# Decay logits of a gated linear attention: one float32r product on stacked high and low parts in place of a float32 product

## The chip, the core and the metric

The kernel runs on 1 core of one Trainium2 chip. The metric is the device time of one execution in microseconds (us), as the median of repeated runs; lower is better. The profile is one further execution, recorded by the hardware profiler. Its engines are PE (the matrix engine; PEld is its weight load), DVE (vector), ACT (scalar), POOL (GpSimd) and SP, which here only issues DMAs.

## The reference, cut to what matters

Two decoder layers work on 1024 tokens of width 1024. Each layer projects its normalised input to three groups of heads (windowed attention, retention, gated linear attention), gates their outputs, and projects back. The change touches only the decay of the gated linear attention: 16 low-rank channels `ga` of every token are multiplied by a 16 x 128 matrix, a bias is added, and the log-sigmoid of that is the log of the decay.

```
def hybrid_layer(x, c_act, positions, ...):
    h = rms_norm(x, pre_gain) * (1.0 + scale) + shift
    (aq, ak, av, ag, rq, rk, rv, rg, gq, gk, gv, gg, ga) = split(h @ w_in)
    ...
    gate_logits = ga @ gla_gate_w + gla_gate_b            # (1024, 16) @ (16, 128)
    log_a = log_sigmoid(gate_logits) / 16
    g = gated_linear_attention(gq, gk, gv, log_a)
    ...
    return x + gate * rms_norm(y, post_gain)
```

## The kernel before, in words

Tokens stand in 8 tiles of 128 (t = 0 to 7). A large product in float32 accuracy is made of three float32r products: both operands are split into a high part (rounded to float32r) and a low part (the rest), and high x high, low x high and high x low are added up in PSUM (`accum`, PASSES). Such matmuls all go through `mult` (L165); transposes go through `transp` (L180).

A layer begins with the gate stage. For each tile, `pre` (L651 to L708) squares the input on ACT, takes the power -1/2 on POOL (`rstd_of`, L634 on DVE and L635 on POOL), scales on DVE (L666), transposes on PE, and splits. Then `do_gates` projects the tile to the gate `gg` together with the 16 channels (272 columns) and to the gate `rg` (256 columns). In layer 0 this goes two tiles at a time, in layer 1 six and then two.

For each `gg` tile a job `gla_logits` (L990) copies the 16 channels from PSUM on ACT (L992), waits a planned time (`gz1`), transposes them on PE to 16 rows, and copies these to `gaT`, a tile of 32 rows x 512 tokens that POOL had set to ones (L781), so that row 16 is a row of ones for the bias. After four tiles a job `gla_log` (L1005) multiplies `gaT` by the weights `gwt` (16 rows of weights, a bias row, zeros): one float32 product of 32 rows x 128 columns with 512 moving columns, twice a layer, four times in all. ACT and DVE make the log-sigmoid of it (L1011 to L1016), and `gla_decays` (L1028) the decays.

`gwt` is a constant, set up before layer 0: DVE clears it (L805) and four DMAs on SP bring weights and bias of both layers (L807, L808).

What sets the order of the work: PE runs in the order in which the program issues its instructions. The small products are jobs (generators) that are resumed inside the long projections, after every 7th matmul (`pump`, CHUNK), when a planned clock `clk` has reached their time. `mult` adds a planned cost to this clock: for 512 columns 0.853 for float32 and 0.213 for float32r. So the planned cost of a product shifts what is issued behind it. The other engines' order is set by a list scheduler of the language. PSUM has three banks for projections (`mm`) and five for the rest (`aux`); SBUF tiles come from pools (`t1`: 8 buffers, `st` for weights on their way in: 5).

Other lines in the prediction: L533, L151 and L149 split loaded weights (low part on DVE or POOL, high part on DVE, high part on ACT); L364 adds up the modulation of the layer on DVE from loaded `w_mod` rows; L986 finishes SiLU of a gate on DVE and so frees the bank; L817 to L822 are the rotation of the retention's q and k on DVE.

Of the kernel before, what the change touches and what calls it, by code (L numbers as in the profile page):

```python
# [10 lines left out]
F32 = mybir.dt.float32  # L11
F32R = mybir.dt.float32r
I32 = mybir.dt.int32
AF = mybir.ActivationFunctionType
ALU = mybir.AluOpType
AX = mybir.AxisListType

P = 128
# [3 lines left out]
NT = S // P  # L22
# [71 lines left out]
def trunk(ctx: ExitStack, tc: tile.TileContext, ins, cst, out):  # L94
    nc = tc.nc
    V, A, G, T = nc.vector, nc.scalar, nc.gpsimd, nc.tensor
    x_in, c_in, pos_in, w_mod, b_mod, pre_g, post_g, w_in, sinks, gw_in, gb_in, gn_in, w_out, w_ga, w_last = [
        ins[n] for n in _INS
    ]

    cp = ctx.enter_context(tc.tile_pool(name="const", bufs=1))
    bp = ctx.enter_context(tc.tile_pool(name="big", bufs=1))
    gp = ctx.enter_context(tc.tile_pool(name="work", bufs=2))
# [5 lines left out]
    def nm(s):  # L109
        uid[0] += 1  # L110
        return f"{s}_{uid[0]}"
# [4 lines left out]
    def t1(dt=F32):  # L116
        return gp.tile([P, 256], dt, tag="t1", name=nm("t1"), bufs=B1)
# [4 lines left out]
    def small(w, dt=F32):  # L122
        return gp.tile([P, w], dt, tag="sm", name=nm("sm"), bufs=BS)
# [4 lines left out]
    def aux(dt=F32):  # L128
        return ps.tile([P, 512], dt, tag="aux", name=nm("aux"), bufs=8 - MMB)

    def f(ap):
        return ap.bitcast(F32)
# [20 lines left out]
    def dma(k, dst, src):  # L153
        {"S": nc.sync, "A": A, "P": G}[EN[k]].dma_start(dst, src)  # L154
# [24 lines left out]
    def transp(dst, src, idn):  # L179
        T.transpose(dst, src, idn)  # L180
        clk[0] += 0.056 if src.dtype == F32R else 0.109

    def lat(key, l):

        return L[key + "@1"] if l and key + "@1" in L else L[key]
# [4 lines left out]
    def flag(name, lat=0.0):  # L190
        flags[name] = clk[0] + lat
# [41 lines left out]
    def cload(name, dt=F32, eng=nc.sync):  # L233
        a = cst[name]
        t = cp.tile(list(a.shape), dt, name="c_" + name)
        eng.dma_start(t, a)
        return t
# [3 lines left out]
    ident = cload("ident", eng=A)  # L241
# [535 lines left out]
    gat = []  # L777

    def new_ga():
        gat.append(gp.tile([P, NT * P], F32, tag="kT1", name=nm("gaT"), bufs=1)[0:32, 0:512])  # L780
        G.memset(gat[-1], 1.0)  # L781
    stR = cp.tile([P, 2, P], F32, name="stR")
    stG = cp.tile([P, 4, 64], F32, name="stG")
    stC = cp.tile([P, 64], F32, name="stC")
# [16 lines left out]
    for l in range(DEPTH):  # L801
        V.tensor_copy(sink8[:, l].rearrange("p (m r) -> p m r", r=2),
                      sinkn[:, 8 * l:8 * l + 8].rearrange("p (r m) -> p m r", r=2))
    gwt = cp.tile([32, 2, P], F32, name="gwt")
    V.memset(gwt, 0.0)  # L805
    for l in range(DEPTH):
        nc.sync.dma_start(gwt[0:16, l, :], gw_in[l])  # L807
        nc.sync.dma_start(gwt[16:17, l, :], gb_in[l:l + 1, :])  # L808
    def rotary(dst, src, nh, t, kind):

        s4 = src.rearrange("p (h c k) -> p h c k", h=nh, c=2)
        sn = sincos[:, t, 0, kind * 32:kind * 32 + 32]
        cs = sincos[:, t, 1, kind * 32:kind * 32 + 32]
        b = gp.tile([P, 256], F32, tag="tr", name=nm("tr"), bufs=1)
        b4 = b[:, 0:nh * 64].rearrange("p (h c k) -> p h c k", h=nh, c=2)
        d4 = dst.rearrange("p (h c k) -> p h c k", h=nh, c=2)
        V.tensor_tensor(d4, s4, cs.unsqueeze(1).unsqueeze(1).to_broadcast((P, nh, 2, 32)), ALU.mult)  # L817
        snb = sn.unsqueeze(1).to_broadcast((P, nh, 32))
        V.tensor_tensor(b4[:, :, 0, :], s4[:, :, 1, :], snb, ALU.mult)
        V.tensor_tensor(b4[:, :, 1, :], s4[:, :, 0, :], snb, ALU.mult)  # L820
        V.tensor_tensor(d4[:, :, 0, :], d4[:, :, 0, :], b4[:, :, 0, :], ALU.subtract)
        V.tensor_tensor(d4[:, :, 1, :], d4[:, :, 1, :], b4[:, :, 1, :], ALU.add)  # L822
# [158 lines left out]
    def silu2(pg):  # L981

        th = t1()
        A.activation(th, pg, AF.Tanh, scale=0.5)
        sg = t1()
        V.scalar_tensor_tensor(sg, th, 1.0, pg, ALU.add, ALU.mult)  # L986
        return sg


    def gla_logits(l, t, pg, pa):  # L990
        ga = small(16)
        A.activation(ga, pa, AF.Copy)  # L992
        dma("ssg", sgS[t], silu2(pg))
        yield lat("gz1", l)
        if t >= 4:
            yield (0.0, ("z", l, 0))
        pt = aux()
        transp(pt[0:16, 0:P], ga, ident)
        A.activation(gat[l][0:16, (t % 4) * P:(t % 4 + 1) * P], pt[0:16, 0:P], AF.Copy)
        flag(("ga", l, t), lat("gz2", l))  # L1000

    las = {}
# [454 lines left out]
    def layer(l):  # L1457
        if l == 0:
            job(table_job())
        new_ga()  # L1460
        def do_gates(name, p):
            w = used(l, name)
            for t in (2 * p, 2 * p + 1):
                pg = mm()
                if name == "gg":
                    project(pg[:, 0:272], l, t, w, 272)
                    job(gla_logits(l, t, pg[:, 0:256], pg[:, 256:272]))
                else:
                    project(pg[:, 0:256], l, t, w)
                    dma("ssr", srS[t], silu2(pg[:, 0:256]))  # L1470
                pump()
            if p == NP_ - 1:
                load(l, "rk" if name == "gg" else "rv")
            if name == "gg" and p % 2:
                job(gla_log(l, p // 2))
# [237 lines left out]
```

## Time and profile before

| | |
|---|---|
| median of 3 runs | 1000.36 us (999.89 to 1002.28) |
| profiled execution, its own time | 1005.29 us |
| its span, first to last instruction | 1003.6 us |
| granted PE clock, mean | 0.989 |
| PE busy | 972.6 us (97%) |
| DVE, ACT, POOL busy | 683.7, 409.0, 234.7 us |
| DMA moved | 148.73 MB, mean 148 GB/s |

A line of a group reads: source line, engine, operation, tile written <- tiles read, shape, count | busy time in us, mean ns of one | idle time of the engine before them and what ended it. For PE the shape begins with the stationary operand, rows*columns. A line of a timeline reads: start, length in us, engine, line, operation, count, and in brackets the idle time before it.

### The profile page before, as it was taken

How to read it: one execution, taken by the hardware profiler on the slowest of the kernel's cores; microseconds unless marked ns; L12 is line 12 of the kernel's file. 1: busy time of each engine (PE TensorE's matmuls, PEld its weight loads, DVE VectorE, ACT ScalarE, POOL GpSimd, SP SyncE). 2: the span in 40 equal slices, each digit the busy share in tenths (PEclk: the TensorE clock that was granted, in tenths of full speed). 3: DMA queues.
4: the chain of work that ended last, by engine and by line, in shares of the span. 5: the costliest groups of instructions: out<-in, count | busy, mean ns of one | idle time of the engine just before them, and what ended most of it. 6: DMA issues, size and time to landing. Idle time of an engine off the chain costs nothing.

```text
span 1003.6 us, 19610 instructions
## 1 busy us (share of the span) xinstructions
PE 972.6 (97%) x7137; PEld 827.5 (82%) x7137; DVE 683.7 (68%) x1680; ACT 409.0 (41%) x1152; POOL 234.7 (23%) x275
## 2 busy tenths in 40 slices
PE   5899999999999999999999999999999999999896
PEld 1599999888998777778889999998999777777675
DVE  3788857678666778654677385775766577566786
ACT  2486312233332656632555332133333267563231
POOL 2310001223320234420122010122332034444000
PEclk8899999999999999999999999999999999999998
DMA  8842513623235355597555241352222435477883
GB/s 306 297 145 79 166 43 102 189 78 121 65 94 172 90 156 168 167 283 234 178 171 166 82 139 32 117 171 68 64 82 88 122 91 153 129 227 237 252 272 132
DMA packets 112172, 148.73 MB, mean 148 GB/s; under 512 B 11998, under 2 KB 63688, under 8 KB 112076
## 3 DMA queue, kind: packets, MB, share of 16 engines
q1 hardware_dynamic: 106380, 137.92, 44.2%
q10 hardware_dynamic: 5696, 9.56, 2.6%
q8 instruction: 56, 0.92, 0.4%
q14 instruction: 40, 0.33, 0.1%
HBM read 109.17 MB, written 36.18 MB: 145 GB/s over the span
## 4 chain that ended last, share of the span: by engine, by line
PE 80%; DMA 8%; DVE 7%; issue 2%; POOL 1%; ACT 1%; SPq 1%; ACTq 0%; POOLq 0%; DVEq 0%
PE mm L165 62%; PE aux L165 14%; PE aux L180 5%; DMA st<-in_w_in_dram 2%; DMA st<-in_w_last_dram 1%; POOL sm L635 1%; DMA xk<-in_x_dram 1%; DMA a<-mixS 1%; DMA t<-aoS 1%; DMA t<-mixF 1%; DVE arena L533 1%; DVE t L328 0%; SPq L154 0%; DMA t<-in_x_dram 0%; DMA t<-xs 0%
## 5 line engine op out<-in xcount | busy, mean ns | idle before, releaser
L165 PE MATMUL mm<-arena 128*128 128x256 f32 (+2 forms) x1824 | 300.0, 318 | 1.8 <-ACT arena L704 1.8
L165 PE MATMUL mm<-arena,arena 128*128 128x256 f32 (+2 forms) x1824 | 299.0, 317 | 0.0
L165 PEld LDWEIGHTS mm<-arena 128*128 128x128 f32 x1824 | 255.3, 191 | 26.6 <-issue 4.1
L165 PEld LDWEIGHTS mm<-arena,arena 128*128 128x128 f32 x1824 | 252.9, 188 | 25.2 <-issue 4.4
L635 POOL TENSOR_TENSOR sm<-sm,mhalf 128x1 f32<-128x1 f32 (+1 forms) x64 | 55.8, 871 | 347.0 <-DVE sm L634 328.4
L165 PE MATMUL mm<-arena,mx 128*128 128x512 f32 (+1 forms) x564 | 132.6, 392 | 3.7 <-ACT kept L1332 3.7
L165 PEld LDWEIGHTS mm<-arena,mx 128*128 128x128 f32 x564 | 103.0, 190 | 28.2 <-ACT kept L1332 4.2
L149 ACT ACTIVATE t<-aux 128x256 f32<-128x256 f32 (+2 forms) x124 | 55.7, 467 | 74.9 <-PE aux L180 63.8
L149 ACT ACTIVATE arena<-st 128x512 fp32r<-128x512 f32 x94 | 55.9, 626 | 54.8 <-DMA st<-in_w_in_dram 19.7
L533 POOL TENSOR_TENSOR arena<-st,arena 128x512 fp32r<-128x512 f32 x31 | 43.3, 1399 | 134.1 <-ACT arena L149 96.8
L923 POOL TENSOR_TENSOR smx<-smx,sm 128x512 f32<-128x512 f32 x32 | 36.5, 1142 | 127.6 <-DVE sm L922 118.4
L533 DVE TENSOR_TENSOR arena<-st,arena 128x512 fp32r<-128x512 f32 x77 | 59.5, 794 | 4.5 <-ACT arena L149 2.4
L919 ACT ACTIVATE smx<-smx,sm 128x129 f32<-128x129 f32 x128 | 49.9, 392 | 28.8 <-DVE sm L916 28.8
L180 PE MATMUL aux<-c_ident,t 128*128 128x128 f32 (+1 forms) x292 | 48.8, 284 | 5.8 <-DVE t L666 5.5
L364 DVE SCALAR_TENSOR_TENSOR acc<-st,c_act,acc 128x512 f32<-128x512 f32 x60 | 45.5, 759 | 12.6 <-DMA st<-in_w_mod_dram 12.0
L180 PEld LDWEIGHTS aux<-c_ident,t 128*128 128x128 f32 (+1 forms) x292 | 35.4, 145 | 13.5 <-DVE t L666 7.4
L698 ACT ACTIVATE t<-aux,mod,mod 128x128 f32<-128x128 f32 x68 | 26.0, 460 | 44.5 <-DVE t L1239 18.3
L165 PEld LDWEIGHTS aux<-t,mx 32*128 32x128 f32 (+1 forms) x896 | 39.5, 187 | 3.9 <-issue 1.9
L967 ACT ACTIVATE t<-aux 128x256 f32<-128x256 f32 x32 | 12.3, 384 | 73.3 <-PE aux L165 60.7
L165 PE MATMUL aux<-t,mx 32*128 32x32 f32 (+1 forms) x896 | 40.6, 272 | 0.0
L914 DVE COPY_PREDICATED smx<-c_curmask,aux 128x256 f32<-128x256 int32 x64 | 25.5, 447 | 18.9 <-ACT smx L149 15.8
L1239 DVE SCALAR_TENSOR_TENSOR t<-t,sm,t 128x512 f32<-128x512 f32 x32 | 23.9, 779 | 17.9 <-DMA t<-in_x_dram 12.3
(220 smaller groups left out, 1378.2 us busy)
## 6 DMA issues: line engine op xcount, KB each, us to landing
st<-in_w_in_dram SPq DMA_DIRECT2D x96, 256.0 KB, 3.7
st<-in_w_mod_dram SPq DMA_DIRECT2D x64, 256.0 KB, 3.0
mx<-mixS SPq DMA_DIRECT2D x20, 512.0 KB, 5.8
mixS<-t SPq DMA_DIRECT2D x72, 128.0 KB, 2.6
st<-in_w_last_dram SPq DMA_DIRECT2D x36, 256.0 KB, 3.7
wm<-in_w_mod_dram SPq DMA_DIRECT2D x12, 512.0 KB, 7.2
t<-in_x_dram SPq DMA_DIRECT2D x24, 256.0 KB, 4.3
t<-tabS SPq DMA_DIRECT2D x16, 256.0 KB, 3.7
```

What stands on the lines that cost most here:

```text
L149: A.activation(dst, src, AF.Copy)
L165: T.matmul(dst, lhsT, rhs, start=start, stop=stop)
L180: T.transpose(dst, src, idn)
L364: V.scalar_tensor_tensor(acc, wt, c_act[:, k:k + 1], acc, ALU.mult, ALU.add)
L533: e.tensor_tensor(lo, st, f(hi), ALU.subtract)
L635: G.tensor_tensor(r, r, mhalf[:, :w], ALU.pow)
L698: A.activation(hf[:, ks], at[kt], AF.Identity, scale=gain, bias=shift)
L914: V.copy_predicated(sv, curmask.unsqueeze(1).to_broadcast((P, 2, P)), pv[:, :, n // P - 1, :])
L919: A.activation(sm[:, h, :], sm[:, h, :], AF.Exp, bias=mx[:, h:h + 1], accum_out=sums[:, h:h + 1])
L923: eng("pn").tensor_tensor(sm[:, :, 0:128], sm[:, :, 0:128], rs.unsqueeze(2).to_broadcast((P, 4, P)), ALU.mult)
L967: A.activation(sq, po, AF.Square)
L1239: V.scalar_tensor_tensor(xt[j], yg[j], r, xt[j], ALU.mult, ALU.add)
```

## The change

The channels are split into a high and a low part on POOL: a tile `ga` of 128 tokens x 3 x 16 gets high, low and high again, by a copy with rounding and a subtraction. The transpose brings 48 rows instead of 16, and `gaT` has 128 rows of float32r, set to ones, of which 48 are overwritten. The weights stand three times on the contracted rows: high, high, low, and the bias twice, as high (row 48 gets the low part in the change's last line, row 49 the high one). So one float32r product of 128 rows gives high x high + low x high + high x low + bias. `gwt` is built from a tile `gwf` of pool `t1`, cleared on POOL, filled by eight DMAs, and rounded and subtracted on POOL.

```
 def new_ga():
-    gat.append(gp.tile([P, NT * P], F32, tag="kT1", ...)[0:32, 0:512])
-    G.memset(gat[-1], 1.0)
+    gat.append(gp.tile([P, NT * P], F32R, tag="kT1", ...)[:, 0:512])
+    G.memset(f(gat[-1]), 1.0)
...
-gwt = cp.tile([32, 2, P], F32, name="gwt")
-V.memset(gwt, 0.0)
+gwt = cp.tile([P, 2, P], F32R, name="gwt")
+gwf = t1()
+G.memset(gwf, 0.0)
 for l in range(DEPTH):
-    nc.sync.dma_start(gwt[0:16, l, :], gw_in[l])
-    nc.sync.dma_start(gwt[16:17, l, :], gb_in[l:l + 1, :])
+    c = slice(P * l, P * l + P)
+    for r in (0, 16, 32):
+        nc.sync.dma_start(gwf[r:r + 16, c], gw_in[l])
+    nc.sync.dma_start(gwf[48:50, c], gb_in[l:l + 1, :].to_broadcast((2, P)))
+gwv = gwf.rearrange("p (l n) -> p l n", l=2)
+G.tensor_copy(gwt, gwv)
+G.tensor_tensor(gwt[32:49], gwv[32:49], f(gwt[32:49]), ALU.subtract)
...
 def gla_logits(l, t, pg, pa):
     ga = small(16)
     A.activation(ga, pa, AF.Copy)
+    g3 = gp.tile([P, 3, 16], F32R, tag="ga", name=nm("ga"), bufs=6)
+    G.tensor_copy(g3[:, 0:3:2], ga.unsqueeze(1).to_broadcast((P, 2, 16)))
+    G.tensor_tensor(g3[:, 1], ga, f(g3[:, 0]), ALU.subtract)
     ...
     pt = aux()
-    transp(pt[0:16, 0:P], ga, ident)
-    A.activation(gat[l][0:16, (t % 4) * P:(t % 4 + 1) * P], pt[0:16, 0:P], AF.Copy)
+    transp(pt[0:48, 0:P], f(g3).rearrange("p a n -> p (a n)"), ident)
+    A.activation(gat[l][0:48, (t % 4) * P:(t % 4 + 1) * P], pt[0:48, 0:P], AF.Copy)
```

More of the change, by code (lines that the diff above doesn't have):

```diff
@@ L779, in new_ga @@
     def new_ga():
-        gat.append(gp.tile([P, NT * P], F32, tag="kT1", name=nm("gaT"), bufs=1)[0:32, 0:512])
-        G.memset(gat[-1], 1.0)
+        gat.append(gp.tile([P, NT * P], F32R, tag="kT1", name=nm("gaT"), bufs=1)[:, 0:512])
+        G.memset(f(gat[-1]), 1.0)
     stR = cp.tile([P, 2, P], F32, name="stR")
```

## The prediction

> **What bounds the kernel now.** I read the page first (busy shares, chain), then what PE waits for, then the stages of the change.
>
> ```profile
> PE 972.6 (97%) x7137; PEld 827.5 (82%) x7137; DVE 683.7 (68%) x1680; ACT 409.0 (41%) x1152; POOL 234.7 (23%) x275
> PE 80%; DMA 8%; DVE 7%; issue 2%; POOL 1%; ACT 1%; SPq 1%; ACTq 0%; POOLq 0%; DVEq 0%
> ```
>
> PE is busy 97% of the span and carries 80% of the chain that ended last. The view of PE's waits has eleven rows, 23.2 us in all; its first two and its last are:
>
> ```profile
> PE aux L180 <- DVE posr L405: 5.8, 1, 5.8
> PE aux L180 <- DVE t L666: 5.5, 3, 4.0
> ...
> PE aux L165 <- DVE t L1170: 0.4, 1, 0.4
> ```
>
> The busy times by stage, for three stretches in which products of the change or their tiles lie:
>
> ```profile
> 60.00:85.00 25.00, 25.00 (x211) 24.93 (x210) 21.30 (x55) 17.58 (x51) 3.06 (x4) 1.00 0.38 121
> 85.00:110.00 25.00, 25.00 (x202) 24.00 (x201) 21.93 (x55) 14.93 (x31) 2.72 (x2) 1.00 0.40 127
> 527.00:571.00 44.00, 43.97 (x361) 43.69 (x360) 21.99 (x52) 17.66 (x52) 5.23 (x6) 1.00 0.36 115
> ```
>
> The columns after the length are PE, PEld, DVE, ACT, POOL, then granted clock (1.00). PE never rests here, so a shorter matmul moves what follows forward, until another engine is late. The candidate is DVE, busy 21.9 of 25 us beside the first product. POOL has much room in time (2.7 to 5.2 us busy), but stands in order.
>
> **The four products.** From PE's timeline, the first and the last of the four and what starts next:
>
> ```profile
> 85.77 1.12 PE L165 MATMUL aux<-gaT,gwt 32*128 32x512 f32 x2
> 86.82 1.14 PE L165 MATMUL mm<-arena,arena 128*128 128x272 f32 x7
> ...
> 600.77 1.12 PE L165 MATMUL aux<-gaT,gwt 32*128 32x512 f32 x2
> 601.82 2.29 PE L165 MATMUL mm<-arena 128*128 128x256 f32 x17
> ```
>
> The float32 product is issued as two matmuls and holds PE from start to next start for 1.05 us, all four times: 4 x 1.05 = 4.2 us. What replaces it is a float32r matmul of 128 rows with 512 columns, as in this group (shapes kept apart):
>
> ```profile
> L165 PE MATMUL mm<-arena,mx 128*128 128x512 f32 x516 | 126.9, 402 | 3.7 <-ACT kept L1332 3.7
> ```
>
> Such a matmul occupies PE for 126.9 / 516 = 0.25 us in a stream; alone it takes 0.40. So 4 x 0.25 = 1.0 us comes back, and **-3.2 us** stays (-2.6 if nothing overlapped). The weight load is 128 columns before and after and lies beside matmuls.
>
> **The sixteen transposes** now have 48 stationary columns for 16; the moving identity is unchanged. The weight loads by their columns:
>
> ```profile
> L165 PEld LDWEIGHTS aux<-t,vd 128*64 128x64 f32 x112 | 8.0, 137 | 4.1
> L180 PEld LDWEIGHTS aux<-c_ident,sm 128*16 128x16 f32 x16 | 1.3, 88 | 0.8 <-issue 0.8
> ```
>
> 16 columns take 88 ns and 64 take 137; between them, 48 take about 121. That is 16 x 0.033 = 0.5 us if it all shows, nothing if it lies under matmuls. PEld is busy 43.69 of 44 us in one stage, so I take **+0.2**. The ACT copy of 48 rows for 16 stands between a transpose and a product that comes several us later: nothing.
>
> **POOL's new work.** Per tile a rounding copy of 32 elements and a subtraction of 16. No such copy is in the trace; the nearest rows are
>
> ```profile
> L1087 POOL TENSOR_TENSOR mx<-t,gs 128x64 f32<-128x64 f32 x8 | 4.2, 531 | 14.5 <-PE aux L165 14.5
> L1053 POOL MEMSET gs<- 128x50 f32 x8 | 1.1, 142 | 11.1 <-DVE stC L1133 11.1
> L1090 POOL TENSOR_TENSOR t<-t,gs 128x256 f32<-128x256 f32 x8 | 6.4, 798 | 0.0
> ```
>
> So 0.14 to 0.53 us for the copy (I take 0.35), 0.5 for the subtraction: 0.85 a tile, 14 us in all, and 1.6 us once for `gwt` (two at 798 ns). Its own end is not on the path: the transpose of a tile comes 6 us and more behind its channels (`gz1` is planned at 11.18 and 15.91). What matters is who stands behind these instructions on POOL. In the built order of the changed program these are the powers of `pre`, whose result DVE (L666) and then PE wait for. In layer 0:
>
> ```profile
> 51.85 0.43 SPq L807 DMA_DIRECT2D gwt<-in_gla_gate_w_dram  x1
> ```
>
> ```profile
> 57.61 0.55 POOL L635 TENSOR_TENSOR sm<-sm,mhalf 128x1 f32<-128x1 f32 x1 [6.82 <-DVE sm L634]
> 60.82 0.56 POOL L635 TENSOR_TENSOR sm<-sm,mhalf 128x1 f32<-128x1 f32 x1 [2.66 <-DVE sm L634]
> ```
>
> The rounding of `gwt` stands between these two powers and waits for the last of eight DMAs. The small DMA just ahead on SP, and where PE takes the second tile's transposes:
>
> ```profile
> sm<-in_attn_sinks_dram SPq DMA_DIRECT2D x1, 8.0 KB, 2.8
> ```
>
> ```profile
> 69.00 1.03 PE L180 MATMUL aux<-c_ident,t 128*128 128x128 f32 x8
> ```
>
> From 51.85, eight issues of about 0.45 end at 55.5; landing in 2.8 us gives 58.3, and two operations more, 59.9: 0.9 us before the second power is wanted. PE takes the transposes only at 69.00, 6 us after DVE would have them ready. I cost it at nothing; without cover it would be the lateness less 7 us. SP's four more issues (1.8 us) push back gate stores and weights for the next units, which are wanted from 90 us on: nothing.
>
> In layer 1 one place has no cover:
>
> ```profile
> 533.57 0.93 POOL L635 TENSOR_TENSOR sm<-sm,mhalf 128x1 f32<-128x1 f32 x1 [2.53 <-DVE sm L634]
> 534.53 0.88 DVE L666 TENSOR_SCALAR t<-t,sm 128x512 f32<-128x512 f32 x2 [0.45 <-POOL sm L635]
> 535.07 0.86 PEld L180 LDWEIGHTS aux<-c_ident,t 128*128 128x128 f32 x8 [0.25 <-DVE t L666]
> ```
>
> PE's transposes start as the first L666 ends. In the new order, the split of tile 0 follows this power directly on POOL and runs beside the L666 pair. How that pair does beside POOL is seen in layer 0:
>
> ```profile
> 46.93 1.27 POOL L533 TENSOR_TENSOR arena<-st,arena 128x512 fp32r<-128x512 f32 x1
> 46.99 1.88 DVE L666 TENSOR_SCALAR t<-mx,sm 128x512 f32<-128x512 f32 x2 [0.45 <-POOL sm L635]
> ```
>
> 1.88 us for 0.88: the pair lost 1.0 us beside a POOL operation of 1.27. The split takes about 0.85 and has a gap between its two parts; the loss is 0.3 to 1.1 us, and PE waits as long. I take **+0.7**. The Trainium skill, page "SBUF — State Buffer", section "Who interferes with whom", says that such a DVE operation and a GpSimd operation exclude each other and that the one that issues first holds the port for its whole length. By that rule the loss would be the whole split, 0.85, where I take 0.7 from the rows; the two rows above agree with it.
>
> **What the shorter product reorders.** `clk` runs 0.64 us less per product, so some jobs move by a chunk of 7 matmuls, and DVE's order changes. Most moves are of one chunk and go both ways: 0 +- 1 us. One I can follow. A mult-add L364 of layer 0 moves ahead of the weight splits:
>
> ```profile
> 96.96 0.35 SPq L154 DMA_DIRECT2D st<-in_w_mod_dram  x1
> ```
>
> ```profile
> st<-in_w_mod_dram SPq DMA_DIRECT2D x64, 256.0 KB, 3.0
> ```
>
> ```profile
> 97.22 1.16 DVE L151 CAST arena<-st 128x512 fp32r<-128x512 f32 x1
> ...
> 100.87 0.42 DVE L986 SCALAR_TENSOR_TENSOR t<-t,mm 128x256 f32<-128x256 f32 x1 [1.09 <-ACT t L984]
> ...
> 106.35 0.27 DVE L820 TENSOR_TENSOR tr<-mm,sincos 128x128 f32<-128x128 f32 x1
> ```
>
> ```profile
> 104.33 0.98 PE L165 MATMUL mm<-arena 128*128 128x256 f32 x7
> 105.18 5.06 PE L165 MATMUL mm<-arena 128*128 128x256 f32 x41
> ```
>
> Its rows are issued at 96.96 and land some 3 us later. Even issued 0.9 earlier they hold DVE until about 99.3 with two splits and L986 queued behind it: L986 at about 101.0, as late as before, though PE is 0.8 us ahead. Behind it stands the rotation that frees, with L820 at 106.6, the bank for PE's second k projection. PE came there after 7 + 17 of the matmuls shown, at 107.3, 0.7 us later; now it has none of that left, or 0.1. So **+0.2** (0 to 1.5; below nothing too, to -0.7, as one L364 less stands in the rotations and ACT no longer waits for a load ahead of the last gate).
>
> **Sum.** -3.2 + 0.2 + 0.7 + 0.2 = -2.1 us. The profiled execution would go from 1005.29 to 1003.2; it lies 0.5% above the median of 1000.36, from which I predict **998.2 us**. Its own range, from the bounds: -3.2 - 0.7 - 1 to -2.6 + 0.5 + 1.1 + 1.5, that is 995.5 to 1000.9.
>
> **The rivals.**
> - *The gain arrives whole.* The split slips through between the two L666, the weight loads hide, the reordering nets nothing: -3.2, **997.1**. For it: PE at 100% in all three stages. Against it: the transposes at 535.07, which wait for L666 without slack.
> - *POOL and DVE fight for the port all along: slower.* If each of the 16 splits delays DVE's scaling, splits and mult-adds by most of its 0.85 us, and PE has no slack, 16 x 0.45 = 7.2 us outweigh the gain: +4.0, **1004.4**. It decides from 3.2 / 16 = 0.2 us of PE time a tile. For it: DVE is busy 85 to 88% ahead of and beside the first product. Against it: most splits meet a POOL and DVE queue with 2 us and more before PE's transposes; in layer 1 DVE is busy 22 of 44 us. The rule of the Trainium skill named above (page "SBUF — State Buffer", section "Who interferes with whom") speaks for this rival.
> - *The change doesn't do what it says.* The product still goes as two matmuls: the gain is zero and the terms above remain: +1.1, **1001.5**. Against it: every float32r product in this kernel goes as one.
>
> **How the numbers follow.** A change of 0.3% (3 us) is about what a measurement of this kernel can tell from none. Chances: forecast 0.49, whole gain 0.30, port fight 0.15, no effect 0.06. Faster by over 0.3% means below 997.36: some 0.2 of the whole gain's 0.30 and 0.11 of the forecast's spread, 0.31. Slower by over 0.3% means above 1003.36: most of the port fight and a tail, 0.14. The rest is 0.55. The range 995.5 to 1002.5 takes in the forecast, the whole gain and the no-effect case, and leaves out the port fight and a tail, 0.17.
>
> **What would show it.** Right: the product as four matmuls in all, next start 0.25 us behind; beside the transposes near 533 a longer L666 pair; PE busy about 3 us less. Wrong: new rows of PE waiting for L666 or POOL in the gate stages; powers on POOL behind a `gwt` rounding that ends after 61 us; eight product matmuls still there; a new wait of PE between 100 and 175 us for a bank.

## The result, and the profile after

The changed kernel ran in 996.31 us as the median of 5 runs (995.68 to 998.17), the kernel before beside it in 1000.78 (999.89 to 1002.28). The ratio is 0.9956, with a 95% interval of 0.9938 to 0.9974: 4.5 us less, between 2.6 and 6.2. A second comparison on another occasion (below) gave 0.9974 (0.9962 to 0.9985), 2.6 us less. The two together, each weighted by the inverse square of its half-width, give **-3.1 us, +-1.0**.

The profiled span is 994.6 us where it was 1003.6. The page of the changed kernel, busy times and chain:

```profile
PE 965.7 (97%) x7133; PEld 824.3 (83%) x7133; DVE 683.2 (69%) x1679; ACT 409.3 (41%) x1152; POOL 246.3 (25%) x310
PE 80%; DVE 7%; DMA 7%; issue 2%; POOL 1%; ACT 1%; SPq 0%; ACTq 0%; POOLq 0%; DVEq 0%
```

PE has four matmuls less, as foreseen, and POOL 35 instructions and 11.6 us more. PE still carries 80% of the chain that ended last. PE is busy 6.9 us less than on the first page; over three profiles with the old product (972.6, 970.3, 971.9) and four with the new one (965.7, 967.4, 965.8, 967.9) it is 4.9 us less on the mean, where about 3 were foreseen. The 9.0 us between the spans are more than the change: the unchanged kernel, profiled once more, has a span of 998.5 us, 5.1 less than the first time. The largest part of these 5.1 us is in one row of PE's waits, here in the repeat of the unchanged kernel and then, with two other rows, in the changed one:

```profile
PE mm L165 <- ACT kept L1332: 1.0, 1, 1.0
```

```profile
PE aux L180 <- DVE t L666: 5.0, 3, 3.2
PE aux L165 <- ACT t L149: 3.0, 3, 1.3
...
PE mm L165 <- ACT kept L1341: 0.5, 1, 0.5
```

The columns are time in all, times, longest. In the first profile of before this wait at the end was 3.7 us (the row is in the prediction); L1332 and L1341 are the same line of the program. It varies from one execution to the next, and is nothing of the change: the changed kernel with a doubled split (below) shows 3.6 us in the same row. PE's waits for L666 are three, 5.0 us in all, where they were three and 5.5. So spans are not compared here, but distances between the same two instructions.

The product in PE's timeline of the changed kernel, the first and the last of the four, with the group ahead and what starts next:

```profile
83.86 1.04 PE L165 MATMUL mm<-arena,arena 128*128 128x272 f32 x7
84.75 0.40 PE L165 MATMUL aux<-gaT,gwt 128*128 128x512 f32 x1
84.98 1.91 PE L165 MATMUL mm<-arena,arena 128*128 128x272 f32 x14
...
596.26 0.50 PE L165 MATMUL aux<-gaT,gwt 128*128 128x512 f32 x1
596.60 2.19 PE L165 MATMUL mm<-arena 128*128 128x256 f32 x17
```

From product start to next start it is now 0.23, 0.23, 0.23 and 0.34 us, 1.03 in all, where it was 4.20. That is 3.17 us. The length column (0.40) is not what the product costs: the next matmul starts 0.17 us before this end.

The three stretches of the prediction, after the change (PE, PEld, DVE, ACT, POOL busy, granted clock):

```profile
60.00:85.00 25.00, 25.00 (x211) 24.92 (x210) 21.51 (x54) 17.21 (x50) 5.95 (x12) 1.00 0.38 121
85.00:110.00 25.00, 25.00 (x210) 24.83 (x209) 24.26 (x62) 15.24 (x30) 5.30 (x6) 1.00 0.51 156
527.00:571.00 44.00, 43.86 (x361) 43.53 (x360) 21.71 (x46) 18.86 (x53) 10.00 (x21) 1.00 0.34 108
```

PE is as full as it was; POOL has 2.6 to 4.8 us more in each; DVE is at 24.3 of 25 us in the second, and still no row of PE waits for it there.

### The profile page after: what moved, and what is told of

Read it like the earlier page. It is cut to its first block, busy times and chain, and to the rows that moved or that the text cites. A ratio compares the mean times of both kernels' runs of the same rounds, so it can differ in the third digit from the quotient of the medians.

```text
span 994.6 us, 19641 instructions
## 1 busy us (share of the span) xinstructions
PE 965.7 (97%) x7133; PEld 824.3 (83%) x7133; DVE 683.2 (69%) x1679; ACT 409.3 (41%) x1152; POOL 246.3 (25%) x310
## 4 chain that ended last, share of the span: by engine, by line
PE 80%; DVE 7%; DMA 7%; issue 2%; POOL 1%; ACT 1%; SPq 0%; ACTq 0%; POOLq 0%; DVEq 0%
PE mm L165 61%; PE aux L165 14%; PE aux L180 5%; DMA st<-in_w_in_dram 2%; POOL sm L635 1%; DMA t<-aoS 1%; DMA st<-in_w_last_dram 1%; DMA xk<-in_x_dram 1%; DVE arena L533 1%; DMA a<-mixS 1%; DVE t L1248 0%; DVE t L328 0%; DMA t<-in_x_dram 0%; DMA t<-xs 0%; DMA mixS<-t 0%
## 5 line engine op out<-in xcount | busy, mean ns | idle before, releaser
L165 PEld LDWEIGHTS mm<-arena,arena 128*128 128x128 f32 x1824 | 252.2, 188 | 24.3 <-issue 3.7
L165 PE MATMUL mm<-arena,mx 128*128 128x512 f32 (+1 forms) x564 | 130.6, 387 | 0.5 <-ACT kept L1341 0.5
L533 POOL TENSOR_TENSOR arena<-st,arena 128x512 fp32r<-128x512 f32 x31 | 42.7, 1378 | 79.7 <-ACT arena L149 72.9
L533 DVE TENSOR_TENSOR arena<-st,arena 128x512 fp32r<-128x512 f32 x77 | 58.0, 775 | 5.2 <-ACT arena L149 3.3
L364 DVE SCALAR_TENSOR_TENSOR acc<-st,c_act,acc 128x512 f32<-128x512 f32 x60 | 46.7, 778 | 16.9 <-DMA st<-in_w_mod_dram 16.5
```

The source lines that it names most:

```text
L165: T.matmul(dst, lhsT, rhs, start=start, stop=stop)
L364: V.scalar_tensor_tensor(acc, wt, c_act[:, k:k + 1], acc, ALU.mult, ALU.add)
L533: e.tensor_tensor(lo, st, f(hi), ALU.subtract)
```

## The experiments

Ten kernels were run. Two theories about the size stood at first. **PRODUCT**: the gain is the shorter hold of four products and hardly anything else. **ORDER**: the cheaper planned cost moves small products by a chunk, and that gives or takes time. Later two more came up: **ROWS** (32 contracted rows cost something beside the float32 passes) and, as the rival from the prediction, **PORT** (the split on POOL slows DVE).

### Order or product

*The unchanged kernel*, to see how far a kernel differs from itself.

> The kernel before, unchanged: a second profile of it. The two profiled spans differ by 9.0 us (1003.6 and 994.6), the medians by only 4.5. Both theories expect the same time as before (ratio 1.000) and a span some 4 us shorter than the first profile's 1003.6, so 999 to 1000, with the missing microseconds spread over the last stretch (from 890 us) rather than in the gate stages.

Measured: 1001.97 us, ratio 1.0007 (0.9990 to 1.0023).

*The kernel before in the order of the changed one.*

```
-        mult(z, gwt[:, l, :], gat[l], True, True)
+        mult(z, gwt[:, l, :], gat[l], True, True, 512 / 2400.0)
```

> The kernel before with only the planned cost of the four products lowered to that of the changed kernel (0.213 us for 0.853), so that PE's issue order becomes the changed kernel's, while the product stays float32 and the channels are not split. Theory PRODUCT (the gain is the PE time of the four products, 3.3 us, and the order is worth nothing): the same as before, within 1 us. Theory ORDER (the moved jobs are worth a good part of the 4.5 us): 1 us or more faster than before.

Measured: 1001.26 us, ratio 1.0002 (0.9988 to 1.0015). The order alone shows no gain, between 1.2 us faster and 1.5 slower.

*The changed kernel in the order of before.*

```
-        mult(z, gwt[:, l, :], gat[l], True, True)
+        mult(z, gwt[:, l, :], gat[l], True, True, 2048 / 2400.0)
```

> The changed kernel with the planned cost of the product left at that of float32 (0.853 us), so that PE's order is that of the kernel before; the product is float32r and the channels are split. Theory PRODUCT: as fast as the changed kernel, 996.3 within 1 us. Theory ORDER: 1 us or more slower than the changed kernel, 997.5 to 998.5.

Measured: 997.28 us, ratio 0.9960 (0.9945 to 0.9976): the gain, 2.4 to 5.5 us, is there without the new order. ORDER falls from both sides; what it could still be worth is less than these intervals.

*The changed kernel, its product in float32 again*, on the same 128 rows, with split, transposes and order left as they are.

```
-        mult(z, gwt[:, l, :], gat[l], True, True)
+        mult(z, f(gwt[:, l, :]), f(gat[l]), True, True, 512 / 2400.0)
```

> The changed kernel with the one product per half sequence issued as float32 again, on the same 128 stacked rows and in the same order on every engine but a few places of DVE. Theory PRODUCT: the product holds PE for 1.05 us again where it holds it 0.23 now, so 4 x 0.82 = 3.3 us come back: 996.3 + 3.3 = 999.6, and the PE timeline is later by 0.8, 1.6, 2.5 and 3.3 us behind the four products. Theory ORDER: no more than 2 us come back, and the time stays below 998.5.

Measured: 1000.77 us, ratio 0.9984 (0.9969 to 0.9999). Of the 4.0 us that the kernel just above gains by its ratio, 1.6 (0.1 to 3.1) stay: more than half of the gain goes with the float32r product, as PRODUCT says, but not all of it. Its float32 product, on 128 rows, also showed a shorter distance to the next matmul than the float32 product on 32 rows of the kernel before. That gave ROWS.

### Rows

*The kernel before, with its float32 product on 128 rows.*

```
-    gat.append(gp.tile([P, NT * P], F32, tag="kT1", ...)[0:32, 0:512])
+    gat.append(gp.tile([P, NT * P], F32, tag="kT1", ...)[:, 0:512])
...
-    gwt = cp.tile([32, 2, P], F32, name="gwt")
+    gwt = cp.tile([P, 2, P], F32, name="gwt")
```

> The kernel before with one thing altered: its float32 product contracts 128 rows (the further rows hold 1 in the moving tile and 0 in the weights) for 32; no split, the same order on every engine. Theory ROWS (the 32 rows themselves cost PE time: the next matmul starts 1.05 us behind a 32-row product, and where 128 rows were multiplied in float32 0.85 behind in the two places that show it): next start 0.85 in all four places, from product 1 to product 2 28.2 us for 28.6, the time 0.8 to 1.5 us under the kernel before. Rival (the gap of that run came from its other changes, or is noise): next start 1.05, 28.6 us, no difference.

The second and third product in its PE timeline:

```profile
113.42 1.02 PE L165 MATMUL aux<-gaT,gwt 128*128 128x512 f32 x2
114.28 0.60 PE L180 MATMUL aux<-c_ident,t 128*128 128x128 f32 x4
...
569.53 1.02 PE L165 MATMUL aux<-gaT,gwt 128*128 128x512 f32 x2
570.39 0.38 PE L180 MATMUL aux<-c_ident,sm 128*16 128x128 f32 x2
```

The distance is 0.86 us in both, where 32 rows took 1.05 (at the first and the fourth the view draws the next group into the pair, and shows no distance). From product 1 to product 2 it is 28.33 us for 28.57. So four times the contracted rows cost PE 0.2 us *less*. The whole time, 1000.96 us, ratio 1.0001 (0.9988 to 1.0015), doesn't show it: it lies between 1.2 us faster and 1.5 slower, so that of the expected gain 0.8 us are possible and 1.5 aren't.

*The changed kernel, its float32r product on 32 rows.*

```
-        mult(z, gwt[:, l, :], gat[l], True, True)
+        mult(z, gwt[0:32, l, :], gat[l][0:32], True, True)
```

> The changed kernel with its float32r product on the first 32 rows alone (leaves out the low part of the weights and the bias); split, transposes and order stay. Theory ROWS, if the cost lies in the switch to 32 rows and back: next start about 0.25 + 0.2 = 0.45 us behind, time 0.8 above the changed kernel. Theory ROWS, if it lies in each float32 pass: next start 0.23, no difference. If it is 0.23 and the run is at the changed kernel's time, the row count of a float32r product is free and the padding to 128 rows brought nothing by itself.

```profile
84.10 1.04 PE L165 MATMUL mm<-arena,arena 128*128 128x272 f32 x7
85.07 0.50 PE L165 MATMUL aux<-gaT,gwt 32*128 32x512 f32 x1
85.50 2.02 PE L165 MATMUL mm<-arena,arena 128*128 128x272 f32 x14
```

Next start 0.43 us behind, in all four places within 0.01, for 0.23 with 128 rows. The product itself also starts later: 0.97 us behind the start of the seven matmuls ahead of it, 0.89 in the changed kernel. Measured: 998.60 us, ratio 0.9989 (0.9978 to 0.9999), 1.2 us above the changed kernel measured beside it; the intervals of the two overlap (0.9962 to 0.9985 there).

*Three products in a row*, on 32 rows (shown) and on 128 rows (the same without `[0:32]`), tell a switch from a slow product. Each was profiled in a single execution, of which only distances are used.

```
-        mult(z, gwt[:, l, :], gat[l], True, True)
+        for c in (None, 0.0, 0.0):
+            mult(z, gwt[0:32, l, :], gat[l][0:32], True, True, c)
```

> The changed kernel whose float32r product contracts the first 32 rows alone (leaves out the low part of the weights and the bias) and is issued three times in a row into the same bank, at no planned cost for the repeats, so the order stays. Read from PE's timeline, product start to next start. One product of 32 rows held PE for 0.43 us, one of 128 rows for 0.23. Theory SWITCH (the 0.2 us are paid where PE goes from 128 rows to 32 and back, once a place): 0.43 + 2 x 0.21 = 0.85. Rival EACH (a product of 32 rows is slower by itself): 3 x 0.43 = 1.29.

> The changed kernel with its product of 128 rows issued three times in a row, at no planned cost for the repeats. Each repeat holds PE for 0.21 to 0.23 us: product start to next start 0.65 to 0.69, with both theories. If it is more, then a repeated weight load or the bank costs something, and the run beside it is to be read against this one.

The first place in each, 32 rows first:

```profile
85.81 0.96 PE L165 MATMUL aux<-gaT,gwt 32*128 32x512 f32 x3
86.69 2.02 PE L165 MATMUL mm<-arena,arena 128*128 128x272 f32 x14
```

```profile
85.69 0.86 PE L165 MATMUL aux<-gaT,gwt 128*128 128x512 f32 x3
86.39 1.91 PE L165 MATMUL mm<-arena,arena 128*128 128x272 f32 x14
```

Three of 32 rows hold PE for 0.88 us (0.88 to 0.89 in the four places), three of 128 rows for 0.70 (0.70, 0.70, 0.71, 0.81). The 0.2 us come once a place and not once a product: 0.85 was expected for SWITCH, 1.29 for EACH. Beside a stream of 128-row matmuls a product of 32 rows pays for going there and back. The Trainium skill, page "TensorEngine Tiling (Array Packing)", section "Key Properties", says that a change of the tiling mode drains the TensorE. The runs fit this, if 32 contracted rows are such a mode (which no trace names), and put 0.2 us on it behind the product and 0.08 ahead of it. The fourth product fits too: it stands behind products of 64 rows, and costs 0.34 us with its 128 rows where the other three cost 0.23.

The weight loads show the same, first in the kernel before, then in the changed one:

```profile
85.77 0.29 PEld L165 LDWEIGHTS aux<-gaT,gwt 32*128 32x128 f32 x2
86.82 0.93 PEld L165 LDWEIGHTS mm<-arena,arena 128*128 128x128 f32 x7 [0.76 <-issue]
```

```profile
84.62 0.19 PEld L165 LDWEIGHTS aux<-gaT,gwt 128*128 128x128 f32 x1
84.75 1.92 PEld L165 LDWEIGHTS mm<-arena,arena 128*128 128x128 f32 x14
```

Around the product of 32 rows neither load runs ahead: its own starts with its matmul (85.77), the next one with the next matmul (86.82). Around the product of 128 rows they start 0.13 and 0.23 us before their matmuls (84.75 and 84.98). The matmuls behind are late as well: the fourteen take 2.02 us behind products of 32 rows and 1.91 behind products of 128 (rows above). So the whole cost is more than the 0.2 us. From the start of the fifth matmul ahead of the product to that of the fifth behind it, read matmul by matmul from the traces, the four places together take 8.79 us before and 5.05 after, 7.57 with a float32 product of 128 rows and 6.29 with a float32r product of 32. Of the 3.7 us that the change gives there, 1.2 are the rows, by either pair (8.79 to 7.57, 6.29 to 5.05), and 2.5 the shorter float32r product.

### The split and the port

*The changed kernel*, not altered, and *the same with every split issued twice*.

```
-        G.tensor_copy(g3[:, 0:3:2], ga.unsqueeze(1)...)
-        G.tensor_tensor(g3[:, 1], ga, f(g3[:, 0]), ALU.subtract)
+        for _ in (0, 1):
+            G.tensor_copy(g3[:, 0:3:2], ga.unsqueeze(1)...)
+            G.tensor_tensor(g3[:, 1], ga, f(g3[:, 0]), ALU.subtract)
```

> The changed kernel, not altered, beside which the other three of this call are read. Theory PRODUCT (four products, 4 x 0.8 us shorter, and hardly anything else): about 997.5, some 3.3 us under the kernel before. Theory PRODUCT PLUS ROWS (a float32 product on 32 rows cost PE something more around it, and the other kernels of the first call show 1.2 to 1.6 us for it): 996.3, 4.5 us under the kernel before.

> The changed kernel with the split of each tile issued twice on GpSimd (16 casts and 16 subtractions more, 0.43 us a tile; the results are the same). Theory COVER (the split lies beside work that PE doesn't wait for; beside the first scaling of layer 1 it costs 0.1 us): within 0.5 us of the changed kernel, transposes behind L666 in layer 1 at most 0.4 later. Rival PORT (each split delays DVE's work by its length and PE has no slack): 16 x 0.43 = 7 us at most, 3 to 4 likely, above the changed kernel, with more waits of PE for DVE in the four gate stretches.

Measured: 997.39 us, ratio 0.9974 (0.9962 to 0.9985), and with the doubled split 997.87, ratio 0.9979 (0.9971 to 0.9988). The difference is 0.5 us, where PORT asked for 3 to 4; the half-widths of the two are 1.2 and 0.9 us, 1.4 together (added in squares). The place in layer 1 that was feared, in the changed kernel and then with the doubled split:

```profile
530.08 0.93 POOL L635 TENSOR_TENSOR sm<-sm,mhalf 128x1 f32<-128x1 f32 x1 [2.53 <-DVE sm L634]
530.97 0.20 POOL L1000 CAST ga<-sm 128x32 fp32r<-128x32 f32 x1
531.04 0.88 DVE L666 TENSOR_SCALAR t<-t,sm 128x512 f32<-128x512 f32 x2 [0.44 <-POOL sm L635]
531.26 0.35 POOL L1001 TENSOR_TENSOR ga<-sm,ga 128x16 fp32r<-128x16 f32 x1
531.58 0.86 PEld L180 LDWEIGHTS aux<-c_ident,t 128*128 128x128 f32 x8 [0.36 <-DVE t L666]
...
533.11 1.29 POOL L533 TENSOR_TENSOR arena<-st,arena 128x512 fp32r<-128x512 f32 x1
533.17 1.90 DVE L666 TENSOR_SCALAR t<-t,sm 128x512 f32<-128x512 f32 x2 [0.66 <-POOL sm L635]
```

```profile
530.38 0.21 POOL L1000 CAST ga<-sm 128x32 fp32r<-128x32 f32 x1
530.45 0.88 DVE L666 TENSOR_SCALAR t<-t,sm 128x512 f32<-128x512 f32 x2 [0.44 <-POOL sm L635]
530.66 0.35 POOL L1000 TENSOR_TENSOR ga<-sm,ga 128x16 fp32r<-128x16 f32 x1
530.99 0.86 PEld L180 LDWEIGHTS aux<-c_ident,t 128*128 128x128 f32 x8 [0.36 <-DVE t L666]
...
531.08 0.32 POOL L1000 CAST ga<-sm 128x32 fp32r<-128x32 f32 x1
...
531.48 0.22 POOL L1000 TENSOR_TENSOR ga<-sm,ga 128x16 fp32r<-128x16 f32 x1
```

The split runs beside the L666 pair, as the prediction said, and the pair takes 0.88 us, as without it; with the second split, which begins 0.25 us before the pair's end (531.08), it does so too. POOL's subtraction is the one that grew, to 0.35 us. The pair right behind it, beside an L533 of 1.29 us, takes 1.90 (in the kernel before 1.91, beside the same L533): the fight for the port is real, but here the long POOL operation wins it and the short ones don't. By the rule of the Trainium skill (page "SBUF — State Buffer", section "Who interferes with whom") whoever issues first holds the port for its whole instruction. The second pair agrees in the main: L533 starts 0.06 us ahead, and of the 1.23 us that it still runs the pair loses 1.02. In the first the rule leaves the cast at most the 0.13 us between 531.04 and its end at 531.17, of which no loss shows (0.88), and the subtraction, which comes while DVE works, has to wait; the trace agrees with that (0.35 us for 0.22).

### Where the time went, all traces together

From the start of the first product to the start of what follows the fourth, one profiled execution each (a distance from one instruction to another, free of what happens at the start and the end):

| kernel | us |
|---|---|
| before, its repeat, before in the new order | 516.1, 515.8, 515.0 |
| after, its repeat, after in the old order, split twice | 511.9, 512.2, 511.7, 511.5 |
| after with a float32r product of 32 rows | 512.2 |
| before with a float32 product of 128 rows, after with one | 514.1, 513.6 (the last distance taken as 0.86; it may be 0.1 longer, as the fourth place is elsewhere) |

The means of the first two rows are 515.6 and 511.8: -3.8 us, with a spread of 1.1 and 0.7 within the rows. The four places of the products account for it: 3.7 us from the fifth matmul ahead to the fifth behind, of which 0.2 lie outside this window (ahead of the first product and behind the fourth). The holds are 3.17 of the 3.7; the rest is what the 32 rows had cost ahead of the product and behind the next start. What is then left is less than the spread. The times agree: -3.1 +- 1.0.

## Why the prediction was right or wrong

The time lies in the range, and the gain comes from the product, as forecast; the size is not the forecast one. The forecast was -2.1 us, measured are -4.5 and -2.6, -3.1 together, and what came true is the first rival, "the gain arrives whole" (-3.2). The range, 7 us wide, took in a change without effect too, so that the time lies in it proves little; the terms are what the runs test. Of the four terms the gain was there, with a part that the working didn't have, and the three costs were not.

- **The product, -3.2.** Right for the hold: 4.20 us became 1.03, where 1.0 was predicted (with some luck: three of the four hold PE shorter than the 0.25 us assumed, the fourth longer). What the working had wrong is its sentence that the weight load "lies beside matmuls" before as after: around the 32 rows it doesn't. By the distances, the 0.82 us that one product gave split into 0.63 for float32r (0.86 to 0.23) and 0.19 for the rows (1.05 to 0.86); a further 0.14 us a place, ahead of the product and behind the next start, wasn't in the sum at all. By the four places the whole term is -3.7, 1.2 of it the rows.
- **The transposes, +0.2.** Nothing shows. The weight load of 48 columns takes 103 ns (estimated: 121, for 88 with 16 columns), and two transposes hold PE for 0.14 us, 568.37 to 568.51, as they did before, 572.80 to 572.94:

```profile
L180 PEld LDWEIGHTS aux<-c_ident,ga 128*48 128x48 f32 x16 | 1.6, 103 | 0.1
```

- **The L666 pair beside the split, +0.7.** This is the step that failed. Place and order were right (the cast starts 0.07 us before the pair), the price was not; the longer L666 pair that was named as a sign didn't come (0.88 us). From the power on POOL to the pair it is 0.96 us, and from the pair to PE's transposes 0.55, both before and after. The loss is nothing, and at most 0.1 over the whole stage (from the first gate matmul to these transposes 7.96 us before, 8.06 after). The price was scaled from a POOL operation of 1.27 us on 512 columns, and charged both parts of the split to DVE, though by the rule quoted beside it only the part that issues ahead of the pair can hold it. The split is much shorter than I took it for, in the undisturbed case 0.21 + 0.22 us for 0.85:

```profile
L1000 POOL CAST ga<-sm 128x32 fp32r<-128x32 f32 x16 | 6.8, 427 | 46.3 <-ACT sm L998 46.1
L1001 POOL TENSOR_TENSOR ga<-sm,ga 128x16 fp32r<-128x16 f32 x16 | 4.7, 293 | 1.3
```

  The means here, 427 and 293 ns, are above the medians of 211 and 223: some of the sixteen take longer beside DVE, one cast as long as 1.16 us. It is POOL that waits, and PE has no wait in its view from 527 to 620 us.
- **The rounding of `gwt`, 0.** Right for PE, with room: it ends at 58.6 us, not at 59.9, and the next power comes at 60.16.

```profile
56.78 0.55 POOL L635 TENSOR_TENSOR sm<-sm,mhalf 128x1 f32<-128x1 f32 x1 [2.95 <-DVE sm L634]
57.28 0.40 POOL L813 CAST gwt<-t 128x256 fp32r<-128x256 f32 x1
57.76 0.79 POOL L814 TENSOR_TENSOR gwt<-t,gwt 17x256 fp32r<-17x256 f32 x1
```

  DVE did pay here. The pair beside these two operations, before and after:

```profile
58.30 0.88 DVE L666 TENSOR_SCALAR t<-t,sm 128x512 f32<-128x512 f32 x2
```

```profile
57.39 1.44 DVE L666 TENSOR_SCALAR t<-t,sm 128x512 f32<-128x512 f32 x2
```

  It lost 0.56 us, under the cover that the prediction counted on: PE has no wait between 56 and 66 us.

- **L364 ahead of the splits, +0.2.** The move came as read, and cost nothing. The mult-add waits 0.59 us for its rows and ends at 97.91; the SiLU behind it (L986 before, L992 now) starts at 99.04, 14.29 us after the first product, where it was 15.10 before: as much earlier as PE is, not "as late as before". PE has no wait for a bank there: its 41 matmuls take 5.07 us, before 5.06.

```profile
97.16 0.75 DVE L364 SCALAR_TENSOR_TENSOR acc<-st,c_act,acc 128x512 f32<-128x512 f32 x1 [0.59 <-DMA st<-in_w_mod_dram]
```

- **The rivals.** PORT, as a cost to PE, fell with the doubled split. That the change does nothing fell with the four matmuls less. The whole gain had a chance of 0.30 and the forecast 0.49; the difference between them was three costs, the largest of them scaled from a much longer neighbour in the trace.

What stays open: whether the change gives 2.6 or 4.5 us. The first comparison of the two kernels rests on five runs of each and is the far one; the traces put 3.7 us on the four places, and the two intervals overlap from 2.6 to 3.8. Open too is the share of the rows in the time: the traces give 1.2 us, but the kernel before with 128 rows was no faster in its time (1.0001).

## What to carry to other kernels

On an engine that never rests, price a shortened instruction from its start to the next one's start: the hold came out within 0.03 us here, while its length in the profile would have been 0.17 us too long for each. The weight loads around it belong to the price: where they don't run ahead, as with the 32 rows, there is more to gain than the hold. A cost that lies on an engine with slack should be scaled to the size of the new instruction, not taken from the nearest large one; issuing the suspected instruction twice shows quickly whether it costs anything. A lone product on 32 rows in a stream of 128-row products is better padded to 128 rows (0.3 us a place in these traces; the times alone don't settle it).

## What the hardware showed that was not expected

- A float32r product of 512 columns in a stream of 128-row matmuls holds PE for 0.23 us with 128 rows and for 0.43 with 32; in float32 it is 0.86 and 1.05. Fewer rows cost more, for the switch, and three 32-row products in a row pay it once (0.88 us). With what is lost ahead and behind, the 32 rows cost 0.3 us a place (1.2 in four).
- A cast of 128x32 takes POOL 0.21 us and a subtraction of 128x16 0.22 in most of the sixteen places; beside DVE the same cast took up to 1.16 (1.52 in the repeat).
- A DVE pair of 0.88 us lost nothing beside POOL operations of 0.2 to 0.35 us, 0.56 beside one of 0.40 and one of 0.79, and 1.02 beside one of 1.29.
